# Starting an attention block's second projection inside the hand-ordered opening, with buffers of its own, in a one-core encoder kernel

## The chip, the cores and the metric

The kernel runs on one core of a Trainium2 chip. The core has four compute engines that run side by side and meet at semaphores: TensorE (PE in the profile, its weight loads PEld), VectorE (DVE), ScalarE (ACT) and GpSimd (POOL). SyncE (SP) issues the transfers. The metric is the device time of one execution in microseconds (us). Data that the engines work on lies in SBUF; matmul results land in PSUM, in banks of 2 KB per partition.

## What is computed

A trunk of four residual layers on 512 frames of width 1024, in fp32: pooling mixer, gated MLP, chunked attention with 16 heads, gated MLP. Cut to what matters here:

```python
h = rmsnorm(x, mix_norm[i])
x = x + chunk_attention(h, w_qkv, q_norm, k_norm, rel_table, w_o)   # odd layers
# in it:
qkv = h @ w_qkv
q, k, v = split(qkv, 3)             # q and k: head_rmsnorm, per head
s = q k^T * scale + bias            # then softmax, then p @ v, then @ w_o
# and ahead of it, as behind every mixer:
x = x + (silu(causal_dwconv3(h W_gate)) * (h W_val)) W_out
```

## The kernel before

**Products in parts.** Every fp32 operand of a matmul is split into a hi part (rounded to the type `fp32r`) and a lo part (the rest): ScalarE copies the operand into the hi part, then another engine subtracts it from the raw value to get the lo part. `mm3` (lines 121 to 125) makes a product from three matmuls: hi x hi (L123), lo x hi (L124), hi x lo (L125). So each operand costs a ScalarE copy and a subtraction ahead of its matmuls, and most waits of TensorE are waits for such a part.

**The end of the first MLP** (`output`, lines 785 to 830). The hidden channels are multiplied with `W_out` in four groups. In the last group of layer 0 (`last`, m = 5 blocks of hidden channels) eight output blocks d = 0 to 7 of 128 channels are made one after the other: 15 matmuls into a bank of PSUM, then VectorE adds the bank to `X[d]` (L828). During block d, ScalarE makes the hi part of block d+1's weights (L797); VectorE makes the lo part (`w[d + 1][2]()`, L798) from where TensorE's order has reached the third of the five. Two hooks of the attention block run in here. `after(d - 1)` comes ahead of the matmuls of block d, `amid(d)` ahead of its third set of matmuls. `after` turns the finished block into what the attention needs: `scaled` (three ScalarE instructions: scaled frame values, their hi part, their square), `low` (lo part, VectorE), `add_square`, and every second block `frame_sums` (four VectorE instructions, L957 to L960) and `forms_hi` and `forms_lo` (hi and lo parts of those sums). It also asks for weights (`ask`, `block`).

**The opening of the attention** (`opening`, lines 931 to 1268). Its instructions on TensorE, VectorE, ScalarE and SyncE stay in the order in which the code writes them (`manual_schedule`); GpSimd's are placed by the framework's planner. It makes a first projection of q and k channels (`project(kk)` for four quarters kk of the contraction, whose weights' parts are `q0` to `q3`), then the values v by a Strassen-like scheme in fourteen steps `half(0)` to `half(13)`, each with a hi part (`hi(n)`, L989) and a lo part (`lo(n)`, L992) of its weights. The results stay in two banks at a time (`A`, tag Q; `B`, tag P), and are added up (`add`, L1160) and stored as `V` (`store`: four pairs of a ScalarE hi part, L107, and a VectorE lo part, L108). The opening ends with

```python
half(12, A, "s4", False)
store(y6[0], 2, 0)
half(13, A, "s4", False)
c = pair_of("c12")
nc.scalar.activation(c[0], A[0], AF.Copy)
nc.vector.tensor_copy(c[1], A[1])      # L1264
store(y6[1], 3, 0)
for i in range(2):
    store(c[i], i, 1)
```

**The second projection** (`project(1)` of line 1283, another function of the same name) is a generator that gives one matmul per step, 96 in all: four quarters of 24. Its four results lie in PSUM banks P, P, Q, Q, so the first two need the banks of `B` and the last two those of `A`. `products` loads each quarter with `load_split`: the raw weights into one of three buffers (`wr`), the hi part by ScalarE (L102), the lo part by GpSimd (L103), each into one of two buffers (`wh`, `wl`) that the opening's parts use as well. All raw buffers of the opening's last steps (`b22r`) are among the three.

**The attention loop** (lines 1429 to 1475). For 64 tiles (16 heads of four) it issues scores, turns and mixes. Between them `fill` takes matmuls from a list of fillers, each with its number and the stretch of tiles over which they are spread; the first is `(project(1), 96, -3, 3.5)`. `fill(0)` ahead of the first tile thus takes 45 of the 96. Here only TensorE's order is fixed; the planner places ScalarE's, VectorE's and GpSimd's instructions by its own simulated times, and it may set them between those of the opening.

Of the kernel before, what the change touches and what calls it, by code (L numbers as in the profile page):

```python
# [23 lines left out]
P = 128  # L24
# [48 lines left out]
def trunk(ctx: ExitStack, tc: tile.TileContext, xt, xT, cols, band, edge, poolw, gv, wout, wqk, wv, wo, rel, out):  # L73
# [289 lines left out]
    def ffn(l, first, pool, acc, summed=None, upool=None, hook=None):  # L363
# [421 lines left out]
        def output(g):  # L785
# [24 lines left out]
            for d in range(KD):  # L810
                if d + 1 < KD:
                    halves(d + 1)
                if last and d:
                    hook["after"](d - 1)
                o = psum("Q", f"out{l}_{g}_{d}")
                for i in range(m):
                    if last and i == 2:
                        hook["amid"](d)
                    if i == 2 and d + 1 < KD:
                        w[d + 1][2]()  # L820
                        if d + 1 + ahead < KD:
                            ask(g, d + 1 + ahead)
                        elif d + 2 == KD and g + 2 < len(OUT):
                            ask(g + 1, 0)
                    s = slice(i * P, (i + 1) * P)
                    yield from mm3(o, w[d][0][:, s], w[d][1][:, s], *slot[b + i], i == 0, i == m - 1)
                for fs in (slice(0, S),) if l == 0 or g < len(OUT) - 1 or d < KD - 1 else (slice(0, HALF), slice(HALF, S)):
                    nc.vector.tensor_add(X[d][:, fs], o[:, fs], X[d][:, fs])  # L828
                    if l == 1 and g == len(OUT) - 1:
                        nc.sync.dma_start(out[d * P:(d + 1) * P, fs], X[d][:, fs])  # L830
# [83 lines left out]
    def attention(rest, hook, hidden_slots):  # L914
# [16 lines left out]
        def opening(pre):  # L931
# [91 lines left out]
            def lo(n):  # L1023
                part_lo(f"v{n}")


            def after(d):
                if d in (3, 5):
                    forms_hi((d - 3) // 2)
                scaled(d)  # L1030
                if d == 6:
                    part_hi("q0")
                if d == 1:
                    low(0)
                if d == 2:
                    low(1)
                if d > 1:
                    add_square(d - 1)
                if d in (2, 4, 6):
                    frame_sums(d // 2 - 1)  # L1040
                if d in (3, 5):
                    forms_lo((d - 3) // 2)
                if 3 < d < KD - 1:
                    ask(d - 4)
                if d > 3:
                    for n in (("b11", "b12"), ("b22",), ())[d - 4]:
                        for j in range(2):
                            block(n, j)

            def amid(d):  # L1050
                if d == KD - 1:
                    part_lo("q0")

            hook["after"], hook["amid"] = after, amid
# [10 lines left out]

            def project(kk):
                h, l = part[f"q{kk}"]
                for c, t in [(c, t) for c in range(2) for t in range(TT)] if kk < 3 else [(c, t) for t in range(TT) for c in range(2)]:
                    k = 2 * kk + c
                    q, s = slice(t * P, (t + 1) * P), slice(c * S, (c + 1) * S)  # L1070
                    run(mm3(ov[t], XS[k][:, q], XS[KD + k][:, q], h[:, s], l[:, s], k == 0, k == KD - 1))
# [36 lines left out]
            frame_sums(3)  # L1108
            project(0)
            part_hi("q2")  # L1110
# [5 lines left out]
            t1(0)  # L1116
            project(1)
            part_hi("q3")
# [4 lines left out]
            t2(0)  # L1123
            project(2)
            st = psum("P", "n1_st")
# [12 lines left out]
            lo(0)  # L1138
            project(3)

# [106 lines left out]
            lo(11)  # L1247
            B = [psum("P", f"vd{i}") for i in range(2)]
            half(10, B, "a22", True)
            hi(12)  # L1250
# [4 lines left out]
            hi(13)  # L1255
            lo(13)
            add(y6, B)
            store(y5[1], 3, 1)
            half(12, A, "s4", False)
            store(y6[0], 2, 0)  # L1260
            half(13, A, "s4", False)
            c = pair_of("c12")
            nc.scalar.activation(c[0], A[0], AF.Copy)
            nc.vector.tensor_copy(c[1], A[1])  # L1264
            store(y6[1], 3, 0)
            for i in range(2):
                store(c[i], i, 1)
            return rcol

        def products(ov, w, name, eng=None, evict=None):  # L1270

            for kk in range(4):
                hi, lo = load_split(w[kk], 1024, f"{name}_{kk}", eng=eng)

# [7 lines left out]

        def project(c, banks="PQ"):

# [18 lines left out]

            yield from products(ov, wqk[c], f"wqk{c}", nc.gpsimd, evict)

# [114 lines left out]
        with tc.tile_pool(name="pre", bufs=1, reuse_waits="tile") as pre:  # L1420
            with tc.manual_schedule(engines={ET.PE, ET.DVE, ET.Activation, ET.SP}):
                rcol = opening(pre)
        heads = closing.enter_context(tc.tile_pool(name="bh", bufs=1, reuse_waits="tile"))
# [6 lines left out]
        nb = len(tiles_)  # L1430
        fillers = [(project(1), 96, -3, FE[0]), (project(2), 96, FE[0], FE[1]), (project(3), 96, FE[1], FE[2]), (outputs(), 144, FE[2], nb + FO)]

# [137 lines left out]
```

## Time and profile before

| | us |
|---|---|
| median of three runs | 974.8 (973.29 to 975.76) |
| the profiled execution | 974.83 |
| its span, first to last instruction | 973.0 |
| mean granted TensorE clock | 0.998 |
| share of the span with ScalarE busy | 61% |
| share with GpSimd busy | 10% |

The span is that of one profiled execution. Times in lines of the trace count from the span's start. In a line of the timeline the first number is the start, the second the duration, then engine, line of the code, operation, output<-inputs by the program's names, shapes and count; in brackets the idle time of that engine just ahead, and what ended it. A line of several instructions gives the stretch from the first start to the last end. A busy TensorE row includes the pipeline's depth (0.39 us for a 128x512 matmul that starts every 0.23 us), so TensorE's losses are read from start to start. In a row of the windows stand the length, then TensorE, its weight loads, VectorE, ScalarE and GpSimd (busy us and instructions), the granted TensorE clock, the share of the transfer engines, and GB/s.

### The profile page before, as it was taken

The page shows a single profiled execution, that of the slowest core. Times are in us where ns is not written, and L with a number is a line of the kernel's source. Part 1 is how long each engine was busy: PE and PEld are TensorE (multiplying, and loading weights), DVE is VectorE, ACT ScalarE, POOL GpSimd, SP SyncE. Part 2 cuts the span into 40 slices and gives each one's busy share as a digit, 9 for nine tenths or more (in the row PEclk, how much of TensorE's full clock was granted, in tenths as well). Part 3 has the DMA queues.
Part 4 walks back from the last instruction along what each step waited for, and adds up shares of the span by engine and source line. Part 5 has one row for each costly group of instructions (what it writes and reads, how often), then busy time and mean ns, then how long its engine had stood idle before and what let it go on. Part 6 is the DMA issues. An engine that isn't in the chain of part 4 may idle for free.

```text
span 973.0 us, 13739 instructions
## 1 busy us (share of the span) xinstructions
PE 959.5 (99%) x4958; PEld 811.5 (83%) x4958; DVE 849.5 (87%) x1520; ACT 593.5 (61%) x1023; POOL 96.5 (10%) x83
## 2 busy tenths in 40 slices
PE   8999999999999999998999999999999999999998
PEld 7788988888888877886888787888988888888886
DVE  8999999999899859894677888999999999989953
ACT  7665565654555556464899888646565565556531
POOL 2300000000000000033534443000000000000000
PEclk9999999999999999999999999999999999999999
DMA  8222332332323417013333341332332233322323
GB/s 342 79 90 71 114 114 74 120 119 92 104 76 119 117 41 293 32 44 118 115 116 113 96 115 57 100 93 94 92 115 88 99 122 97 115 99 82 110 80 113
DMA packets 38997, 103.87 MB, mean 107 GB/s; under 512 B 4465, under 2 KB 7937, under 8 KB 38929
## 3 DMA queue, kind: packets, MB, share of 16 engines
q1 hardware_dynamic: 38864, 102.95, 32.7%
q8 instruction: 39, 0.64, 0.3%
q14 instruction: 30, 0.24, 0.1%
q0 software_dynamic: 32, 0.04, 0.0%
q10 hardware_dynamic: 32, 0.00, 0.0%
HBM read 96.65 MB, written 2.14 MB: 102 GB/s over the span
## 4 chain that ended last, share of the span: by engine, by line
PE 92%; DVE 5%; ACT 2%; issue 1%; DMA 0%; DVEq 0%
PE st_m L593 11%; PE out L125 8%; PE out L124 8%; PE out L123 8%; PE st_m L595 6%; PE st_t L593 6%; PE gv L124 4%; PE gv L123 4%; PE gv L125 4%; PE qk L123 3%; PE qk L124 3%; PE qk L125 3%; PE st_t L595 3%; PE st_b L593 3%; DVE one L108 2%; PE tp L1398 2%
## 5 line engine op out<-in xcount | busy, mean ns | idle before, releaser
L124 PE MATMUL out<-one,ow_h 128*128 128x512 f32 x224 | 88.1, 393 | 0.0
L123 PE MATMUL out<-one,ow_h 128*128 128x512 f32 x224 | 88.0, 393 | 0.0
L125 PE MATMUL out<-one,ow_l 128*128 128x512 f32 x224 | 87.9, 393 | 0.0
L828 DVE TENSOR_TENSOR X<-out,X 128x512 f32<-128x512 f32 (+1 forms) x65 | 44.1, 679 | 46.7 <-PE out L125 46.5
L593 PE MATMUL st_m<-two,g_h 128*128 128x512 f32 x240 | 75.0, 394 | 0.0
L593 PE MATMUL st_m<-h,g_h 128*128 128x512 f32 x240 | 74.1, 390 | 0.0
L392 ACT ACTIVATE ow_h<-wo_r 128x768 fp32r<-128x768 f32 (+1 forms) x56 | 44.5, 794 | 43.4 <-PE out L124 40.9
L407 DVE SCALAR_TENSOR_TENSOR c<-a,col,c 128x511 f32<-128x511 f32 (+1 forms) x76 | 56.2, 742 | 0.0
L593 PEld LDWEIGHTS st_m<-h,g_h 128*128 128x128 f32 x240 | 45.1, 188 | 10.3
L595 PEld LDWEIGHTS st_m<-two,g_l 128*128 128x128 f32 x240 | 45.1, 188 | 9.6
L602 ACT ACTIVATE w<-st_m 128x512 f32<-128x512 f32 x30 | 17.9, 598 | 57.1 <-PE st_m L595 57.1
L593 PEld LDWEIGHTS st_m<-two,g_h 128*128 128x128 f32 x240 | 44.1, 188 | 10.1 <-ACT w L602 0.8
L393 DVE TENSOR_TENSOR ow_l<-wo_r,ow_h 128x768 fp32r<-128x768 f32 (+1 forms) x56 | 49.9, 891 | 2.1 <-ACT ow_h L392 2.1
L595 PE MATMUL st_m<-h,g_l 128*128 128x256 f32 x240 | 48.3, 283 | 0.0
L1386 DVE CUSTOM_DVE_ANT_0 sb<-sc,B 128x128 f32<-128x128 f32 (+1 forms) x64 | 31.0, 485 | 19.6 <-PE sc L1383 11.6
L595 PE MATMUL st_m<-two,g_l 128*128 128x256 f32 x240 | 47.6, 280 | 0.0
L124 PEld LDWEIGHTS out<-one,ow_h 128*128 128x128 f32 x224 | 42.4, 189 | 5.6 <-DVE one L418 0.3
L125 PEld LDWEIGHTS out<-one,ow_l 128*128 128x128 f32 x224 | 42.4, 189 | 5.5
L123 PEld LDWEIGHTS out<-one,ow_h 128*128 128x128 f32 x224 | 42.4, 189 | 5.4
L404 ACT ACTIVATE c<-a,col 128x512 f32<-128x512 f32 x38 | 30.7, 812 | 23.2 <-DVE a L751 21.6
L123 PE MATMUL qk<-wqk_h,two 128*128 128x512 f32 x96 | 40.7, 424 | 2.6 <-DVE c L1264 2.6
L1388 ACT ACTIVATE sb<-sb,mx 128x128 f32<-128x128 f32 (+1 forms) x64 | 35.7, 557 | 10.4 <-DVE mx L1386 9.9
(456 smaller groups left out, 3031.3 us busy)
## 6 DMA issues: line engine op xcount, KB each, us to landing
gv_r<-gv SPq DMA_DIRECT2D x86, 512.0 KB, 3.9
wo_r<-wout SPq DMA_DIRECT2D x32, 384.0 KB, 3.1
wo_r<-wout SPq DMA_DIRECT2D x32, 320.0 KB, 2.9
wqk_r<-wqk SPq DMA_DIRECT2D x12, 512.0 KB, 3.4
b<-wv SPq DMA_DIRECT2D x8, 512.0 KB, 6.1
wo_r<-wo SPq DMA_DIRECT2D x8, 512.0 KB, 3.3
xt<-xt SPq DMA_DIRECT2D x4, 512.0 KB, 5.2
X<-xT SPq DMA_DIRECT2D x8, 256.0 KB, 7.4
```

The source lines that it names most:

```text
L123: yield nc.tensor.matmul(o, sh, mh, start=first, stop=False, **how)
L124: yield nc.tensor.matmul(o, sh, ml, start=False, stop=False, **how)
L125: yield nc.tensor.matmul(o, sl, mh, start=False, stop=last, **how)
L392: nc.scalar.activation(hi[:, :n], raw[:, :n], AF.Copy)
L393: return hi, lo, lambda: nc.vector.tensor_sub(lo[:, :n], raw[:, :n], hi[:, :n].bitcast(F32))
L404: nc.scalar.activation(c, a, AF.Identity, scale=cw[2], bias=cw[3])
L407: nc.vector.scalar_tensor_tensor(c[:, j:], a[:, :S - j], cw[2 - j], c[:, j:], op0=OP.mult, op1=OP.add)
L593: nc.tensor.matmul(o, hi[:, c], B[i, name], start=first and i == 0, stop=False, **how)
L595: nc.tensor.matmul(o[:, 0], lo[:, c], B[i, name][:, 0], start=False, stop=i == 3, **how)
L828: nc.vector.tensor_add(X[d][:, fs], o[:, fs], X[d][:, fs])
L1386: nc.vector.tensor_tensor_reduce(out=s_[:, :n], in0=sc[:, :n], in1=BT[h % 2][:, :n][:, ::-1], scale=1.0, scalar=3e38, op0=OP.add, op1=OP.m ...
L1388: nc.scalar.activation(s_[:, :n], s_[:, :n], AF.Exp, scale=-1.0, bias=mx[:, 0:1], accum_out=mx[:, 1:2])
```

## The change

Three things are changed, all between the last output group of the first MLP and the first tile of the attention loop.

In the last output group, the lo part of the next block's weights comes ahead of `frame_sums` and `forms_lo` in VectorE's order, and `part_hi("q0")` comes ahead of `scaled(6)` in ScalarE's order.

```diff
                     if last and i == 2:
-                        hook["amid"](d)
+                        hook["amid"](d, w[d + 1][2] if d + 1 < KD else None)
                     if i == 2 and d + 1 < KD:
-                        w[d + 1][2]()
+                        if not last:
+                            w[d + 1][2]()
...
             def after(d):
+                if d == 6:
+                    part_hi("q0")
                 if d in (3, 5):
                     forms_hi((d - 3) // 2)
                 scaled(d)
-                if d == 6:
-                    part_hi("q0")
-                if d == 1:
-                    low(0)
-                if d == 2:
-                    low(1)
+                if d in (1, 2):
+                    low(d - 1)
                 if d > 1:
                     add_square(d - 1)
-                if d in (2, 4, 6):
-                    frame_sums(d // 2 - 1)
-                if d in (3, 5):
-                    forms_lo((d - 3) // 2)
...
-            def amid(d):
-                if d == KD - 1:
+            def amid(d, low_part):
+                if low_part:
+                    low_part()
+                else:
                     part_lo("q0")
+                d -= 1
+                if d in (2, 4, 6):
+                    frame_sums(d // 2 - 1)
+                if d in (3, 5):
+                    forms_lo((d - 3) // 2)
```

The opening's own `project(kk)` is renamed `query(kk)`. The second projection's generator is started in the opening. Its first quarter gets two buffers of the pool `pre` for its parts (`then`), which ScalarE and VectorE make in the fixed order, and 24 of its matmuls are issued behind `half(13)`. The copies of the last bank come ahead of the stores of `y6`.

```diff
             lo(11)
             B = [psum("P", f"vd{i}") for i in range(2)]
+            raw = load(wqk[1, 0], "wqk1_0_r")
+            then = [pre.tile([P, 1024], F32R, name=f"wqk1_0_{v}", tag="pre", bufs=8) for v in "hl"]
             half(10, B, "a22", True)
...
             hi(13)
             lo(13)
+            nc.scalar.activation(then[0], raw, AF.Copy)
             add(y6, B)
+            nc.vector.tensor_sub(then[1], raw, then[0].bitcast(F32))
+            half(12, A, "s4", False)
             store(y5[1], 3, 1)
-            half(12, A, "s4", False)
-            store(y6[0], 2, 0)
             half(13, A, "s4", False)
             c = pair_of("c12")
             nc.scalar.activation(c[0], A[0], AF.Copy)
             nc.vector.tensor_copy(c[1], A[1])
-            store(y6[1], 3, 0)
+            second = project(1, ready=then)
+            for _ in range(24):
+                next(second)
+            for i in range(2):
+                store(y6[i], 2 + i, 0)
             for i in range(2):
                 store(c[i], i, 1)
-            return rcol
+            return rcol, second
```

`products` takes the ready parts for quarter 0 in place of `load_split`, and the first filler holds the other 72 matmuls, over a stretch that begins later.

```diff
-                hi, lo = load_split(w[kk], 1024, f"{name}_{kk}", eng=eng)
+                hi, lo = ready if ready and kk == 0 else load_split(w[kk], 1024, f"{name}_{kk}", eng=eng)
...
-        fillers = [(project(1), 96, -3, FE[0]), (project(2), 96, FE[0], FE[1]), (project(3), 96, FE[1], FE[2]), (outputs(), 144, FE[2], nb + FO)]
+        fillers = [(second, 72, -1.35, FE[0]), (project(2), 96, FE[0], FE[1]), (project(3), 96, FE[1], FE[2]), (outputs(), 144, FE[2], nb + FO)]
```

More of the change, by code (lines that the diff above doesn't have):

```diff
@@ L1064, in opening, with query @@
             A = [psum("Q", f"va{i}") for i in range(2)]
-            def project(kk):
+            def query(kk):
                 h, l = part[f"q{kk}"]
@@ L1108, in opening @@
             frame_sums(3)
-            project(0)
+            query(0)
             part_hi("q2")
@@ L1116, in opening @@
             t1(0)
-            project(1)
+            query(1)
             part_hi("q3")
@@ L1123, in opening @@
             t2(0)
-            project(2)
+            query(2)
             st = psum("P", "n1_st")
@@ L1138, in opening @@
             lo(0)
-            project(3)
+            query(3)
             ss, a, y, t_ = norms_of(0)
@@ L1264, in opening, with products @@
             nc.vector.tensor_copy(c[1], A[1])
-            store(y6[1], 3, 0)
+            second = project(1, ready=then)
[3 more added lines that the diff above has]
+                store(y6[i], 2 + i, 0)
             for i in range(2):
                 store(c[i], i, 1)
-            return rcol
-        def products(ov, w, name, eng=None, evict=None):
+            return rcol, second
+        def products(ov, w, name, eng=None, evict=None, ready=None):
             for kk in range(4):
-                hi, lo = load_split(w[kk], 1024, f"{name}_{kk}", eng=eng)
+                hi, lo = ready if ready and kk == 0 else load_split(w[kk], 1024, f"{name}_{kk}", eng=eng)
                 for c, t in [(c, t) for c in range(2) for t in range(TT)] if kk < 3 else [(c, t) for t in range(TT) for c in range(2)]:
@@ L1281, in products, with project @@
                         evict(t)
-        def project(c, banks="PQ"):
+        def project(c, banks="PQ", ready=None):
             ov = [psum(banks[t // 2], f"qk{c}_{t}", BANKS[banks]) for t in range(TT)]
@@ L1302, in evict @@
                 late.append(lambda: squares(t))
-            yield from products(ov, wqk[c], f"wqk{c}", nc.gpsimd, evict)
+            yield from products(ov, wqk[c], f"wqk{c}", nc.gpsimd, evict, ready)
             def norms():
@@ L1421, in attention @@
             with tc.manual_schedule(engines={ET.PE, ET.DVE, ET.Activation, ET.SP}):
-                rcol = opening(pre)
+                rcol, second = opening(pre)
         heads = closing.enter_context(tc.tile_pool(name="bh", bufs=1, reuse_waits="tile"))
```

## The prediction

> **What bounds the kernel now.** I read the page first (busy shares, chain), then TensorE's waits, then the order of time on each engine around those waits.
>
> ```profile
> PE 959.5 (99%) x4958; PEld 811.5 (83%) x4958; DVE 849.5 (87%) x1520; ACT 593.5 (61%) x1023; POOL 96.5 (10%) x83
> ...
> PE 92%; DVE 5%; ACT 2%; issue 1%; DMA 0%; DVEq 0%
> ```
>
> TensorE is busy 959.5 of 973.0 us, so an edit that leaves its matmuls alone can gain only at places where TensorE waits. The waits of TensorE between 330 and 460 us, the stretch the diff touches (us in total, times, longest):
>
> ```profile
> PE qk L123 <- DVE c L1264: 2.6, 1, 2.6
> PE qk L124 <- POOL wqk_l L103: 1.2, 1, 1.2
> PE qk L124 <- DVE q_l L992: 0.8, 1, 0.8
> PE out L125 <- DVE ow_l L798: 0.3, 1, 0.3
> PE qk L123 <- ACT q_h L989: 0.2, 1, 0.2
> ```
>
> Five waits at two places: the last three at the end of the first gated MLP ("the front"), the first two where the second projection begins ("the seam"). Their full price is read from TensorE's starts, about 0.23 us apart when nothing is late.
>
> **The front, part by part.** TensorE in order of time (start, duration):
>
> ```profile
> 361.73 0.40 PE L124 MATMUL out<-u0l,ow_h 128*128 128x512 f32 x1
> 362.41 0.50 PE L125 MATMUL out<-u0h,ow_l 128*128 128x512 f32 x1 [0.28 <-DVE ow_l L798]
> ...
> 375.78 0.39 PE L125 MATMUL out<-one,ow_l 128*128 128x512 f32 x1
> 376.35 0.51 PE L123 MATMUL qk<-q_h,two 128*128 128x512 f32 x1 [0.18 <-ACT q_h L989]
> 377.61 0.50 PE L124 MATMUL qk<-q_l,two 128*128 128x512 f32 x1 [0.75 <-DVE q_l L992]
> ```
>
> The three steps are 0.68, 0.57 and 1.26 us instead of 0.23: lost are 0.45 + 0.34 + 1.03 = 1.82 us. What each waits for, on VectorE and ScalarE:
>
> ```profile
> 360.07 0.42 DVE L957 TENSOR_TENSOR s<-y,y 128x256 f32<-128x256 f32 x1
> ...
> 361.54 0.82 DVE L798 TENSOR_TENSOR ow_l<-wo_r,ow_h 128x640 fp32r<-128x640 f32 x1
> ...
> 372.06 0.61 ACT L944 ACTIVATE n_sq<-X 128x512 f32<-128x512 f32 x1
> ...
> 375.26 1.04 ACT L989 ACTIVATE q_h<-wqk 128x1024 fp32r<-128x1024 f32 x1
> ...
> 373.92 0.42 DVE L957 TENSOR_TENSOR s<-y,y 128x256 f32<-128x256 f32 x1
> ...
> 376.33 1.23 DVE L992 TENSOR_TENSOR q_l<-wqk,q_h 128x1024 fp32r<-128x1024 f32 x1 [0.86 <-ACT q_h L989]
> ```
>
> - lo part of `ow` ahead of the frame sums: the four sums stand from 360.07 to 361.54. With the lo part at 360.07 it is done at 360.9; TensorE wants it at 361.96. The 0.45 go.
> - `part_hi("q0")` ahead of `scaled(6)`: ScalarE is free at 372.7, and the buffer that q0 takes over is free once the next-to-last bank has read it, about then. So q_h is done near 373.7 instead of 376.3, and q_l, now behind the square's addition and ahead of the sums, runs from 373.9 to 375.1. The last bank ends at 376.01 less 0.45 = 375.56. The 0.34 and the 1.03 go.
> - What is late next: these sums start 1.2 us later, then the forms made of them, then q1's parts. No instruction is added; lo parts and sums change places. q1's lo part, at 379.40 to 380.6 now, is wanted 24 x 0.23 = 5.5 us after 375.56, at 381.0: about a microsecond to spare. The quarters behind it keep 0.5 to 1.5 us by the same count. SP issues the same transfers at the same points of its order.
>
> Does the gain reach the seam? VectorE itself waits for TensorE ahead of it:
>
> ```profile
> 400.42 0.69 DVE L1176 COPY z<-qk 128x512 f32<-128x512 f32 x1 [1.89 <-PE qk L125]
> 410.00:420.00 10.00, 10.00 (x47) 8.21 (x46) 9.90 (x12) 5.28 (x7) 6.84 (x4) 1.00 0.01 2
> ```
>
> 1.89 us of idle absorb what VectorE is behind. From there to the seam VectorE is full (9.90 of 10 us in the second row, columns PE, PEld, DVE, ACT, POOL), but its start moves with TensorE. I take 1.8 us for the front; bounds 0 (VectorE eats it) and 1.82.
>
> **The seam.** TensorE, VectorE, POOL and ScalarE now:
>
> ```profile
> 439.39 0.39 PE L123 MATMUL qk<-wqk_h,two 128*128 128x512 f32 x1
> 440.96 0.50 PE L124 MATMUL qk<-wqk_l,two 128*128 128x512 f32 x1 [1.18 <-POOL wqk_l L103]
> ...
> 442.68 0.39 PE L125 MATMUL qk<-wqk_h,two 128*128 128x512 f32 x1
> 445.69 0.80 PE L123 MATMUL qk<-wqk_h,two 128*128 128x512 f32 x1 [2.62 <-DVE c L1264]
> ...
> 449.07 0.40 PE L125 MATMUL qk<-wqk_h,two 128*128 128x512 f32 x1
> ...
> 437.46 1.28 DVE L1160 TENSOR_TENSOR y<-y,vd 128x512 f32<-128x512 f32 x2
> 438.65 6.38 DVE L108 SCALAR_TENSOR_TENSOR one<-y,n_y,one 128x128 fp32r<-128x128 f32 x8
> 444.96 0.68 DVE L1264 COPY c<-va 128x512 f32<-128x512 f32 x1
> ...
> 438.54 4.78 POOL L103 TENSOR_TENSOR wqk_l<-wqk_r,wqk_h 128x1024 fp32r<-128x1024 f32 x2 [12.89 <-ACT wqk_h L102]
> ...
> 435.24 1.05 ACT L989 ACTIVATE v_h<-b22r 128x1024 fp32r<-128x1024 f32 x1
> 436.19 1.26 ACT L107 ACTIVATE one<-y,n_y 128x128 fp32r<-128x128 f32 x4
> 439.48 1.04 ACT L102 ACTIVATE wqk_h<-wqk_r 128x1024 fp32r<-128x1024 f32 x1
> ```
>
> From 439.39 to 449.07 are 17 steps, 3.86 us at the 0.227 of undisturbed steps: 5.82 us are lost. 1.34 wait for POOL's lo part, 2.78 for the copy of the last bank, and the rest is a slower clock (PEclk is the column behind POOL):
>
> ```profile
> 446.00:447.00 1.00, 1.00 (x3) 0.81 (x3) 1.00 (x5) 0.95 (x4) 0.00 (x0) 0.50 0.82 304
> 427.83 1.13 DVE L108 SCALAR_TENSOR_TENSOR one<-x,n_y,one 128x128 fp32r<-128x128 f32 x4
> 433.45 0.35 SPq L117 DMA_DIRECT2D wqk_r<-wqk  x1
> wqk_r<-wqk SPq DMA_DIRECT2D x7, 512.0 KB, 3.4
> ```
>
> At a granted 0.50 the 8 steps from 445.69 took 3.38 us instead of 1.82: 1.56. The copy is late because eight store instructions stand ahead of it in 6.38 us; four of them take 1.13 us elsewhere. In between POOL runs two lo parts of 2.4 us, and VectorE hardly gets an instruction through: the two engines hold each other up. [...]
>
> After the change, on the clock of before (all of it comes 1.8 us earlier):
> - The first quarter's raw load is asked behind `channel_major`'s moves, near 427, and lands 3.4 us later. `then[0]` follows hi(13) on ScalarE: 436.2 to 437.2.
> - `then[1]`, on VectorE instead of POOL, comes behind the two additions: 438.74 to 439.95 (1.2 like q_l above). The second matmul wants it at 439.62: a stall of 0.35.
> - ScalarE then makes store(y5[1]) until 438.4. The second quarter's hi part is not in the fixed order; its raw load (433.45 + 3.4) has landed at 436.9. ScalarE is idle until the last bank ends at 439.5, so I put it there, at 438.4, and POOL's lo part behind it from 439.9, when `then[1]` is through, to 442.3.
> - Four store instructions, not eight, now stand ahead of the copy. The first is blocked until 442.3, the others follow; the copy starts at 443.2, and the tenth matmul at 443.95 (0.73 after the copy's start, as now) instead of 445.69.
> - The gap is then 443.95 - 441.8 = 2.15 us, against 2.78. The clock fell behind 2.78 and not behind 1.34. I take it as staying full, since the gap is shorter and TensorE worked just before.
>
> Gain: 445.69 - 443.95 = 1.74, and 1.56 of clock: **3.3 us**. Bounds for the unseen POOL place: the copy unblocked at 441.1 leaves only the 0.35 (gain 5.82 - 0.35 = 5.47); both lo parts in its way again leaves about nothing.
>
> The rest is covered. The planner of matmuls emits 24 of the second projection in the opening and 21 ahead of the first scores, 45 as now. The second quarter is wanted near 447.4 and ready at 442.3. The 16 stores behind the copy (16 x 0.28 from 443.9, and 2.4 for one more POOL part) end near 450.8; VectorE's first need comes later and has room:
>
> ```profile
> 455.96 0.29 DVE L1386 CUSTOM_DVE_ANT_0 sb<-sc,B 128x128 f32<-128x128 f32 x1 [7.17 <-issue]
> PE wo L124 <- DVE two L103: 0.7, 1, 0.7
> PE oo L1410 <- DVE pt1l L103: 0.5, 1, 0.5
> PE tp L1398 <- ACT sb L1390: 0.5, 2, 0.3
> ```
>
> The last three rows are all of TensorE's waits from 449 to 700: behind the seam TensorE alone sets the pace, and what is gained stays.
>
> **Sum.** 1.8 + 3.3 = 5.1 us against 974.83, the profiled execution (span 973.0, 1.8 around it; the median shown is 974.8, the same): **969.7 us**.
>
> **Rivals.**
> 1. POOL's lo part comes behind the copy: 974.83 - 1.8 - 5.47 = **967.6**. For it: ScalarE's queue is filled by a planner whose clock is not the chip's. Against: the idle place ahead of the last copy exists. Chance 0.20.
> 2. The clock falls again, 1.56 us dearer: **971.3**. For: it fell behind 2.78 us. Against: not behind 1.34. Chance 0.13. [...]
> 3. VectorE, full, eats the front's gain: 974.83 - 3.3 = **971.5**. The 1.89 us of idle speak against. Chance 0.05.
> 4. The second quarter's hi part stands behind all stores on ScalarE. No lock then, the copy ends near 441.7, but 16 stores of 0.3 (the row at 436.19) from 440.1 end at 444.9, hi at 445.9, POOL at 448.4 where 445.2 is wanted: 0.35 + 3.2 + 1.56 lost instead of 5.82, the front kept: **972.3**. Chance 0.05.
> 5. Slower: in the attention loop the order of VectorE and ScalarE is planned anew, and each of 16 heads' `mix` waits for its lo part as one does now (0.5): 8.0 - 5.1, **977.7**. It outweighs the gain from 0.32 us a head. For: ScalarE has few gaps there. Against: 0.5 in all now, since parts are made two tiles ahead. Chance 0.07.
>
> My forecast has 0.50; with it goes POOL's lo part getting ahead of `then[1]`, which stalls the second matmul until 441.95 and costs nearly the same (969.6).
>
> **Chances.** A measurement of this kernel tells some 0.3% (2.9 us) from no change. Faster: the forecast, rival 1 and half of 2, 0.77. Within: the other half, 3 and 4, 0.16. Slower: 0.07. The range, 967.0 to 972.5, reaches from just under rival 1 to just over rival 4.
>
> **What would show it.** TensorE's list of waits loses ow_l L798, q_l L992 and q_h L989; q_h precedes y L941 in ScalarE's order; a 128x1024 subtraction at the seam is VectorE's; the copy of the last bank follows four stores; a wait of some 2 us for it remains, with a POOL part beside it, and PEclk stays 1.00. Wrong would be: any of the three still there, the copy unblocked (rival 1), a clock of 0.50 (2), or new waits at oo (5).

## The result and the profile after

The changed kernel takes 969.56 us (median; 969.34 to 969.78, 4 executions) against 975.09 us before (973.29 to 975.76, 4 executions, one more than in the table above): a ratio of 0.9946, 95% interval 0.9929 to 0.9963. The profiled execution after took 969.34 us with a span of 967.5 us, 5.49 us less than the profiled one of before.

The page of the changed kernel, busy time by engine and the shares of the chain that ended last:

```profile
PE 957.4 (99%) x4958; PEld 810.7 (84%) x4958; DVE 850.8 (88%) x1521; ACT 593.7 (61%) x1023; POOL 94.6 (10%) x82
...
PE 94%; DVE 3%; ACT 2%; issue 0%; DMA 0%; DVEq 0%
```

One subtraction went from POOL to VectorE (83 to 82 instructions, 1520 to 1521), TensorE does as many matmuls as before, and VectorE's share of the chain falls from 5% to 3%. TensorE's waits of the changed kernel between 330 and 700 us (total, times, longest):

```profile
PE qk L123 <- DVE c L1269: 1.7, 1, 1.7
PE wo L124 <- DVE two L103: 0.6, 1, 0.6
PE oo L1419 <- DVE pt1l L103: 0.5, 1, 0.5
PE tp L1407 <- ACT sb L1399: 0.5, 2, 0.3
```

Of the five waits at the front and the seam one is left, that for the copy of the last bank. The other three rows are those that already stood behind the seam, the same to 0.1 us: the attention loop was not replanned for the worse (rival 5).

The end of the first MLP in the timeline of the changed kernel (start, duration), TensorE, VectorE, ScalarE:

```profile
361.61 0.40 PE L124 MATMUL out<-u0l,ow_h 128*128 128x512 f32 x1
361.85 0.40 PE L125 MATMUL out<-u0h,ow_l 128*128 128x512 f32 x1
...
375.12 0.39 PE L125 MATMUL out<-one,ow_l 128*128 128x512 f32 x1
375.35 0.39 PE L123 MATMUL qk<-q_h,two 128*128 128x512 f32 x1
375.58 0.39 PE L124 MATMUL qk<-q_l,two 128*128 128x512 f32 x1
...
359.96 0.82 DVE L798 TENSOR_TENSOR ow_l<-wo_r,ow_h 128x640 fp32r<-128x640 f32 x1
...
373.27 1.22 DVE L993 TENSOR_TENSOR q_l<-wqk,q_h 128x1024 fp32r<-128x1024 f32 x1
...
371.92 1.04 ACT L990 ACTIVATE q_h<-wqk 128x1024 fp32r<-128x1024 f32 x1
372.86 0.71 ACT L942 ACTIVATE y<-X,col 128x512 f32<-128x512 f32 x1
```

The three steps that were late are 0.23 to 0.24 us now. The lo part of `ow` runs 1.6 us earlier than before, and q_h and q_l are done over a microsecond before TensorE wants them.

The seam in the timeline of the changed kernel, TensorE, VectorE, POOL, ScalarE:

```profile
437.30 0.39 PE L123 MATMUL qk<-wqk_h,two 128*128 128x512 f32 x1
437.77 0.50 PE L124 MATMUL qk<-wqk_l,two 128*128 128x512 f32 x1
...
439.51 0.40 PE L125 MATMUL qk<-wqk_h,two 128*128 128x512 f32 x1
441.56 0.50 PE L123 MATMUL qk<-wqk_h,two 128*128 128x512 f32 x1 [1.66 <-DVE c L1269]
...
443.51 0.39 PE L125 MATMUL qk<-wqk_h,two 128*128 128x512 f32 x1
...
436.50 1.22 DVE L1263 TENSOR_TENSOR wqk_l<-wqk_r,wqk_h 128x1024 fp32r<-128x1024 f32 x1
437.63 3.27 DVE L108 SCALAR_TENSOR_TENSOR one<-y,n_y,one 128x128 fp32r<-128x128 f32 x4
440.83 0.68 DVE L1269 COPY c<-va 128x512 f32<-128x512 f32 x1
441.43 4.32 DVE L108 SCALAR_TENSOR_TENSOR one<-y,n_y,one 128x128 fp32r<-128x128 f32 x8
...
437.33 2.64 POOL L103 TENSOR_TENSOR wqk_l<-wqk_r,wqk_h 128x1024 fp32r<-128x1024 f32 x1 [13.84 <-PE va L1096]
442.21 2.61 POOL L103 TENSOR_TENSOR wqk_l<-wqk_r,wqk_h 128x1024 fp32r<-128x1024 f32 x1 [2.23 <-ACT wqk_h L102]
...
436.15 1.05 ACT L102 ACTIVATE wqk_h<-wqk_r 128x1024 fp32r<-128x1024 f32 x1
```

VectorE makes the first quarter's lo part; four stores, lengthened from 1.13 to 3.27 us by the POOL part beside them, stand ahead of the copy; the copy holds up the tenth matmul. From the first to the eighteenth matmul the seam takes 443.51 - 437.30 = 6.21 us instead of 9.68. Behind the gap the clock is full (the stretch in the windows of the changed kernel; PEclk behind POOL):

```profile
446.00:447.00 1.00, 1.00 (x6) 0.84 (x5) 1.00 (x6) 0.00 (x0) 0.00 (x0) 1.00 0.42 130
```

**Where the 5.5 us of span come from:** 0.12 us of difference stands already at 347 us, ahead of everything that was changed; 1.91 comes at the front (from the `u0l` matmul at 347.76 us before and 347.64 after to the first q_l matmul, at 377.61 and 375.58, are 29.85 and 27.94 us); 3.47 at the seam. The two matmuls from which the front is counted, in the kernel before and in the changed one:

```profile
347.76 0.40 PE L124 MATMUL out<-u0l,ow_h 128*128 128x512 f32 x1
...
347.64 0.40 PE L124 MATMUL out<-u0l,ow_h 128*128 128x512 f32 x1
```

Of the seam's, 2.04 lies up to the tenth matmul (445.69 - 439.39 = 6.30, now 441.56 - 437.30 = 4.26), and 1.43 in the eight steps behind it (3.38, now 1.95), which is the clock.

No edit of this document changes the code ahead of that matmul, yet in the twelve profiled executions shown here it starts at 347.62 to 349.48 us. So below, what an edit is worth at the seam is checked against steps inside an execution, since a difference of two spans may hold up to 1.9 us of something else.

In the sections below, "gap" is TensorE's step to the matmul that waits for the copy, less the 0.23 us of an undisturbed step: 2.78 us before, 2.05 - 0.23 = 1.82 after. "Half clock" is the stretch of a granted 0.50 behind a gap; in the trace of before it lasts 3.4 us, from 445.4 to 448.8, and begins 0.3 us ahead of the matmul that ends the gap. It shows in a whole execution too: those 3.4 us at 0.50 take 0.0017 off the mean granted clock of a span of 973 us, so a mean of 0.998 or less is read here as an execution with it, and 0.999 or more as one without.

### The profile page after: what moved, and what is told of

It reads as the page before. It is cut to its first block, busy times and chain, and to the rows that moved or that the text cites. A ratio compares the mean times of both kernels' runs of the same rounds, so it can differ in the third digit from the quotient of the medians.

```text
span 967.5 us, 13741 instructions
## 1 busy us (share of the span) xinstructions
PE 957.4 (99%) x4958; PEld 810.7 (84%) x4958; DVE 850.8 (88%) x1521; ACT 593.7 (61%) x1023; POOL 94.6 (10%) x82
## 4 chain that ended last, share of the span: by engine, by line
PE 94%; DVE 3%; ACT 2%; issue 0%; DMA 0%; DVEq 0%
PE st_m L593 11%; PE out L124 8%; PE out L123 8%; PE out L125 8%; PE st_m L595 6%; PE st_t L593 6%; PE gv L124 4%; PE gv L123 4%; PE gv L125 4%; PE qk L123 3%; PE qk L124 3%; PE qk L125 3%; PE st_t L595 3%; PE st_b L593 3%; PE tp L1407 2%; PE oo L1419 2%
```

## Experiments

Each kernel was timed in five rounds against the kernel before on the same chip; a result is the median, the range and the number of executions, then the ratio to the kernel before with its 95% interval. E1 to E4, E5 to E8, and E9 and E10 ran on three chips. On each of them the executions of the kernel before without the half clock have a median of 973.64 to 973.66 us, so that times may be compared from one to another. Diffs are against the changed kernel unless another is named. The theory on trial is the prediction's own: a front term, a copy that is late because of the stores and POOL ahead of it, and a clock that falls behind a long gap. Its rivals here: that one edit carries it all, that VectorE eats the front's gain, or that the own buffers, not the place of the copy, make the seam.

**E1, the front alone.** The opening's end, the generator and the fillers as in the kernel before:

```diff
-            nc.scalar.activation(then[0], raw, AF.Copy)
             add(y6, B)
-            nc.vector.tensor_sub(then[1], raw, then[0].bitcast(F32))
-            half(12, A, "s4", False)
             store(y5[1], 3, 1)
+            half(12, A, "s4", False)
+            store(y6[0], 2, 0)
             half(13, A, "s4", False)
...
-        fillers = [(second, 72, -1.35, FE[0]),
+        fillers = [(project(1), 96, -3, FE[0]),
```

> Only the front is changed (lo part of the next weights ahead of the frame sums, q0's parts ahead of scaled(6)); the second projection starts as before. Theory (two separate gains that add): the three waits at ow_l, q_h and q_l go, TensorE is some 1.9 us earlier at the seam, the seam's loss of 5.8 us stays with its half clock: 975.1 - 1.9 = 973.2. Rival (VectorE is full, the front's gain is eaten on the way to the seam): 975.1, with new waits of TensorE between 376 and 437.

Measured: 973.01 us (971.49 to 974.33, 12); 0.9981 [0.9973, 0.9990]. TensorE's waits of E1 between 330 and 460 us:

```profile
PE qk L123 <- DVE c L1266: 2.6, 1, 2.6
PE qk L124 <- POOL wqk_l L103: 1.2, 1, 1.2
```

The forecast's front term alone gives 974.83 - 1.8 = 973.0. The three waits of the front are gone, the two of the seam as long as before. The front took the same 27.94 us as after, and from there to the first matmul of the second projection it is 61.67 us (61.78 before, 61.72 after), so VectorE does not eat the gain. The range is wide for a reason that the clock shows: eight of the twelve executions have a mean granted clock of 0.998 or less and took 973.0 to 974.3 us, the other four 971.5 to 972.0.

**E2, the seam alone.** `output`, `after` and `amid` as in the kernel before, the rest as changed:

```diff
-                        hook["amid"](d, w[d + 1][2] if d + 1 < KD else None)
+                        hook["amid"](d)
...
-                if d == 6:
-                    part_hi("q0")
                 if d in (3, 5):
                     forms_hi((d - 3) // 2)
                 scaled(d)
+                if d == 6:
+                    part_hi("q0")
```

> Only the seam is changed (own buffers, parts in the fixed order, 24 matmuls in the opening, copies of the last bank ahead of the stores of y6); the front is as before. Theory: the three waits of the front stay (1.9 us), the seam loses 0.2 + 1.8 us and no clock: 975.1 - 3.5 = 971.6. Rival (the two parts need each other, since the seam's ready parts are late when TensorE comes later or earlier): gains of E1 and E2 together differ from 5.5 by more than 1.

Measured: 971.73 us (971.32 to 972.70, 6); 0.9972 [0.9960, 0.9984]. The forecast's seam term alone gives 974.83 - 3.3 = 971.5. The three waits of the front are back at 0.8, 0.3 and 0.2 us, the wait for the copy is 1.7 us, and no execution has a clock under 0.999. Counted from the median of the kernel before on that chip, 974.61 us, E1 and E2 gain 1.6 and 2.9 us. Together that is 4.5 us, a microsecond less than 5.5, which is the mark that the expectation set for its rival. But this median mixes executions with and without the half clock. Counted from those with it alone (975.28 us), E1's with it (973.28) gain 2.0 us and E2 3.55, together 5.55. The steps say the same: E1's front is that of the changed kernel, and E2's gap is 1.84 us against 1.82. So the two halves of the change are separate.

**E3, the copy ahead of the four stores that are left.** The lo parts of `store(y5[1])` move behind the copy on VectorE; ScalarE's order stays:

```diff
             half(12, A, "s4", False)
-            store(y5[1], 3, 1)
+            store(y5[1], 3, 1, False)
             half(13, A, "s4", False)
             c = pair_of("c12")
             nc.scalar.activation(c[0], A[0], AF.Copy)
             nc.vector.tensor_copy(c[1], A[1])
+            store(y5[1], 3, 1, True)
```

(`False` leaves the lo parts out, `True` makes only them.)

> The changed kernel, but VectorE copies the second half of the last bank ahead of the four lo parts of the store of y5[1] too (ScalarE's hi parts stay where they are). POOL's lo part of the second quarter still runs at the same place. Theory (the wait of 1.8 us is the queue of four stores behind POOL's part, ahead of the copy): the copy starts right behind the own lo part, the wait for it goes, TensorE ends 1.8 us earlier, 967.7; the stores end as late as before and nobody waits for them. Rival (the pace behind the seam is set by the stores, or by ScalarE): the wait at the copy goes but comes back later, 969.5.

Measured: 967.54 us (967.41 to 967.89, 4); 0.9926 [0.9913, 0.9939]. VectorE and POOL in the timeline of E3:

```profile
437.69 0.68 DVE L1273 COPY c<-va 128x512 f32<-128x512 f32 x1
438.29 4.79 DVE L1173 SCALAR_TENSOR_TENSOR one<-y,n_y,one 128x128 fp32r<-128x128 f32 x12
...
437.39 2.65 POOL L103 TENSOR_TENSOR wqk_l<-wqk_r,wqk_h 128x1024 fp32r<-128x1024 f32 x1 [13.84 <-ACT wqk_h L102]
442.27 5.15 POOL L103 TENSOR_TENSOR wqk_l<-wqk_r,wqk_h 128x1024 fp32r<-128x1024 f32 x1 [2.24 <-ACT wqk_h L102]
```

The copy, which reads PSUM, takes 0.68 us beside the POOL part (437.39 to 440.04 us), as it does with none beside it (at 440.83 us in the changed kernel), and TensorE has no wait left at the seam. Why it is not held up there and a store is, no run shows. The 2.0 us against the changed kernel are the wait that was left, a gap of 1.82 us.

**E4, POOL's part behind the copy (rival 1 made to happen).** The second quarter's load and hi part may be issued only after ScalarE's copy `c[0]`:

```diff
-            nc.scalar.activation(c[0], A[0], AF.Copy)
+            first_copy = nc.scalar.activation(c[0], A[0], AF.Copy)
...
-            second = project(1, ready=then)
+            second = project(1, ready=then, behind=first_copy)
...
-                hi, lo = ready if ready and kk == 0 else load_split(...)
+                with tc.issue_after(behind.ins) if behind and kk == 1 else nullcontext():
+                    hi, lo = ready if ready and kk == 0 else load_split(...)
```

> The changed kernel, but the second quarter's hi part (and so POOL's lo part) is put behind the copy of the first half of the last bank on ScalarE; VectorE's order is untouched, four stores still stand ahead of the copy. Theory (POOL's part is what holds the first of the four stores for some 2.1 us): the four stores take 1.1 us instead of 3.3, the copy ends 2.1 us earlier, no wait for it is left; the second quarter's lo part comes at about 443.4 where 443.2 is wanted, so up to 0.3 us may be lost there: 967.7 to 968.0. Rival (VectorE's own work sets the copy's time, POOL only stands beside it): the four stores still take about 3 us, 969.5.

Measured: 969.65 us (969.17 to 970.70, 5); 0.9949 [0.9937, 0.9961]. No gain over the changed kernel, against 967.7 to 968.0 expected. VectorE, POOL and TensorE in the timeline of E4:

```profile
438.27 1.14 DVE L108 SCALAR_TENSOR_TENSOR one<-y,n_y,one 128x128 fp32r<-128x128 f32 x4
439.32 0.68 DVE L1269 COPY c<-va 128x512 f32<-128x512 f32 x1
439.92 2.18 DVE L108 SCALAR_TENSOR_TENSOR one<-y,n_y,one 128x128 fp32r<-128x128 f32 x8
442.02 1.13 DVE L108 SCALAR_TENSOR_TENSOR one<-c,n_y,one 128x128 fp32r<-128x128 f32 x4
...
445.44 0.50 PE L124 MATMUL qk<-wqk_l,two 128*128 128x512 f32 x1 [1.30 <-POOL wqk_l L103]
```

and the POOL part by itself (the window of E4 from 441 to 444 us):

```profile
441.64 3.74 POOL L103 TENSOR_TENSOR wqk_l<-wqk_r,wqk_h 128x1024 fp32r<-128x1024 f32 x1 [17.52 <-DVE one L108]
```

Half of the theory held: without POOL beside them the four stores take 1.14 us and the copy is not awaited. But the wait moved. VectorE runs twelve more stores without a break until 443.15, and the POOL part that begins at 441.64 is done at 445.38, 2.2 us after that run has ended and not 2.4 after its start. TensorE waits 1.3 us for it.

**E5, eight stores ahead of the copy again.** The own buffers stay; `store(y6[0])` returns ahead of the copies:

```diff
             store(y5[1], 3, 1)
+            store(y6[0], 2, 0)
             half(13, A, "s4", False)
...
-            for i in range(2):
-                store(y6[i], 2 + i, 0)
+            store(y6[1], 3, 0)
```

> The changed kernel with the stores in their old order: store(y6[0]) ahead of the copies again, so eight store instructions, not four, stand ahead of the second copy; own buffers and the 24 matmuls in the opening stay. Theory (POOL's one part costs 2.1 us once, each further store 0.27): the copy comes 1.1 us later than in the changed kernel, 970.6, with a gap of 2.9 us on TensorE, as long as the one before the change, so that some executions also have the half clock (+1.6): single times from 970.6 to 972.2. Rival (the order of copies and stores is what the change gains at the seam, the buffers do little): the whole seam comes back, 973.0, as in E1.

Measured: 975.08 us (974.16 to 976.92, 11); 1.0004 [0.9995, 1.0013]. With the front's gain in it, this seam is slower than that of the kernel before. The expectation, 970.6 to 972.2, missed by 3 us; the rival's 973.0 missed too. The timeline of E5, VectorE, POOL and TensorE:

```profile
438.67 6.41 DVE L108 SCALAR_TENSOR_TENSOR one<-y,n_y,one 128x128 fp32r<-128x128 f32 x8
445.00 0.68 DVE L1270 COPY c<-va 128x512 f32<-128x512 f32 x1
...
438.37 2.64 POOL L103 TENSOR_TENSOR wqk_l<-wqk_r,wqk_h 128x1024 fp32r<-128x1024 f32 x1 [13.84 <-PE va L1096]
442.07 2.34 POOL L103 TENSOR_TENSOR wqk_l<-wqk_r,wqk_h 128x1024 fp32r<-128x1024 f32 x1 [1.06 <-ACT wqk_h L102]
...
445.73 0.80 PE L123 MATMUL qk<-wqk_h,two 128*128 128x512 f32 x1 [4.79 <-DVE c L1270]
```

The eight stores last long enough to meet the third quarter's POOL part as well: two parts stand in the copy's way, as before the change. TensorE's losses of 1.34 and 2.78 us in the kernel before become one gap of 4.95. The mean granted clock is 0.997 or less in all eleven executions.

**E6, the place of the copies alone.** The kernel before, with one move:

```diff
             half(12, A, "s4", False)
-            store(y6[0], 2, 0)
             half(13, A, "s4", False)
...
-            store(y6[1], 3, 0)
+            for i in range(2):
+                store(y6[i], 2 + i, 0)
```

> The kernel before with one edit: the copies of the last bank ahead of the stores of y6. No own buffers, POOL makes the first quarter's lo part as before, the front is as before. Theory (two lo parts of POOL let through hardly two instructions of VectorE, so the copy still waits for the end of the second): four stores fewer are worth 4 x 0.27 = 1.1 us at the copy, and TensorE waits 1.2 us for POOL's first part as before: 974.6 - 1.0 = 973.6, with the half clock in some executions. Rival (the order alone brings most of the seam): 971.5.

Measured: 972.57 us (972.37 to 973.68, 10); 0.9978 [0.9969, 0.9987]. VectorE and TensorE in the timeline of E6:

```profile
438.77 5.34 DVE L108 SCALAR_TENSOR_TENSOR one<-y,n_y,one 128x128 fp32r<-128x128 f32 x4
444.03 0.68 DVE L1263 COPY c<-va 128x512 f32<-128x512 f32 x1
...
444.76 0.50 PE L123 MATMUL qk<-wqk_h,two 128*128 128x512 f32 x1 [1.57 <-DVE c L1263]
```

Four stores behind two POOL parts still take 5.34 us. Counted from the first matmul of the second projection (439.54 us here, 439.39 before), the copy comes 1.08 us earlier than in the kernel before, as expected, and the gap is 1.73 us instead of 2.78. The time is a microsecond better than expected because no execution of ten has a mean clock under 0.999: against the kernel before without the half clock, 973.65 us, E6 gains just the 1.08.

**E7, twelve stores ahead of the copy.** E5, with `store(y6[1])` moved up too:

```diff
             store(y5[1], 3, 1)
+            for i in range(2):
+                store(y6[i], 2 + i, 0)
             half(13, A, "s4", False)
...
-            for i in range(2):
-                store(y6[i], 2 + i, 0)
```

> The changed kernel with both stores of y6 ahead of the copies: twelve store instructions ahead of the second copy. Made to see what a longer gap on TensorE costs. The copy comes 2.1 us later than in the changed kernel, and up to 2.4 more if POOL's next part falls in: gap 3.9 to 6.3 us. Theory (the clock falls to half for some 3 us in a share of the executions that grows with the gap): 971.7 to 974.1 without, 1.6 more with the half clock, in most executions. Rival (the clock does not depend on the gap): a spread as small as in the changed kernel, granted clock 1.000 throughout.

Measured: 976.25 us (975.37 to 977.23, 11); 1.0013 [1.0004, 1.0021], slower than the kernel before. The twelve stores take 7.47 us, 1.1 more than E5's eight, which is four of 0.27 us. TensorE's longer wait in the timeline of E7 (the matmul ahead of it starts at 442.47 us):

```profile
447.60 0.80 PE L123 MATMUL qk<-wqk_h,two 128*128 128x512 f32 x1 [4.73 <-DVE c L1271]
```

The gap, 5.13 - 0.23 = 4.90 us, lies in the 3.9 to 6.3 expected, and all executions have the half clock. The time is still above the expected 971.7 to 974.1 and 1.6 more: a second loss of 1.01 us was not in the sum, the wait for ScalarE's copy, which has four more hi parts ahead of it.

**E8, both first.** E3, and `then[1]` ahead of the additions:

```diff
-            add(y6, B)
             nc.vector.tensor_sub(then[1], raw, then[0].bitcast(F32))
+            add(y6, B)
```

> E3 (copy ahead of all stores on VectorE), and the first quarter's own lo part ahead of the two additions of y6. The second matmul of the projection waits 0.24 us for that lo part in E3; now it is ready and the additions free their banks in time (the first at about 437.0 for 437.3, the second at 437.7 for 438.0). Theory: no wait is left at the seam, 967.3, 0.2 under E3. Rival (the additions come too late for the first matmul): as E3 or 0.3 worse, with a wait of TensorE for y L1162.

Measured: 967.50 us (967.13 to 967.67, 5); 0.9923 [0.9910, 0.9935]. The same as E3 within what can be measured: the step to the second matmul, 0.53 us in E3, becomes 0.31, and that is all.

**E9, E5 with the third quarter's POOL part out of the way.** Tests the reason given for E5's miss: the third quarter's load and hi part are issued only after ScalarE's last store.

```diff
             store(y5[1], 3, 1)
+            store(y6[0], 2, 0)
             half(13, A, "s4", False)
...
-                hi, lo = ready if ready and kk == 0 else load_split(...)
+                with tc.issue_after(hook["stored"].ins) if ready and kk == 2 else nullcontext():
+                    hi, lo = ready if ready and kk == 0 else load_split(...)
```

> E5 again (eight stores ahead of the second copy), but the third quarter's hi part is put behind the last store on ScalarE, so that POOL's second lo part cannot start ahead of the copy. Theory (E5 was 5 us dearer than the changed kernel because the copy, 1.1 us later, fell behind POOL's second part too, 2.3 us, and the long gap brought the half clock every time): the eight stores take 4.3 us instead of 6.4, the copy starts 2 us earlier than in E5, the gap on TensorE is 2.9 us; 970.7 without the half clock, 972.3 with it, both among the executions. Rival (the second half of the eight stores is slow of itself, say by ScalarE's hi parts): 975.0 as E5.

Measured: 972.48 us (971.87 to 973.50, 11); 0.9980 [0.9972, 0.9989]. VectorE in the timeline of E9:

```profile
438.15 4.33 DVE L108 SCALAR_TENSOR_TENSOR one<-y,n_y,one 128x128 fp32r<-128x128 f32 x8
442.40 0.68 DVE L1271 COPY c<-va 128x512 f32<-128x512 f32 x1
```

and TensorE at the gap:

```profile
440.01 0.40 PE L126 MATMUL qk<-wqk_h,two 128*128 128x512 f32 x1
443.14 0.50 PE L124 MATMUL qk<-wqk_h,two 128*128 128x512 f32 x1 [2.73 <-DVE c L1271]
```

The same eight stores take 4.33 us instead of 6.41, and the gap is 3.13 - 0.23 = 2.90 us instead of 4.95. So 2.05 us of E5's miss were the second POOL part. The rest, under a microsecond, is not traced; E5's profiled execution was already 1.0 us later than that of the changed kernel ahead of the front. The gap of 2.9 us brings the half clock in eleven executions of eleven, where some without it were expected.

**E10, the place of the copy without own buffers.** The front, and E3's order of copy and stores; the second projection starts as in the kernel before, POOL making the first lo part:

```diff
-            raw = load(wqk[1, 0], "wqk1_0_r")
-            then = [pre.tile(...) for v in "hl"]
...
-            nc.scalar.activation(then[0], raw, AF.Copy)
             add(y6, B)
-            nc.vector.tensor_sub(then[1], raw, then[0].bitcast(F32))
+            store(y5[1], 3, 1, False)
             half(12, A, "s4", False)
-            store(y5[1], 3, 1)
             half(13, A, "s4", False)
             c = pair_of("c12")
             nc.scalar.activation(c[0], A[0], AF.Copy)
             nc.vector.tensor_copy(c[1], A[1])
-            second = project(1, ready=then)
-            for _ in range(24):
-                next(second)
+            store(y5[1], 3, 1, True)
...
-        fillers = [(second, 72, -1.35, FE[0]),
+        fillers = [(project(1), 96, -3, FE[0]),
```

> The front as changed, and VectorE's copy of the last bank ahead of all stores as in E3, but no own buffers, no fixed order for the first quarter's parts and no matmuls in the opening: POOL makes the first quarter's lo part. Theory (the order of the copies carries the seam; the own buffers are worth only the 1.3 us that TensorE waits for POOL's first lo part, less the 0.3 it waits for the own one): no wait for the copy, one of 1.2 us for wqk_l, 967.5 + 1.0 = 968.5. Rival (own buffers and matmuls in the opening are worth more than that first wait): 970 or above, with other waits.

Measured: 968.69 us (968.49 to 969.04, 5); 0.9942 [0.9928, 0.9956]. TensorE's only wait of E10 between 330 and 460 us:

```profile
PE qk L124 <- POOL wqk_l L103: 1.2, 1, 1.2
```

So the own buffers, with their parts in the fixed order and the 24 matmuls in the opening, are worth 968.69 - 967.54 = 1.15 us beside E3. That is the wait: the step to the second matmul is 1.61 us in E10 and 0.53 in E3. The place of the copy carries the rest of the seam. With the front and nothing else (E1) the time is 973.01: moving the copies alone takes 4.3 us off it, 2.8 of them the gap and the other 1.5 the half clock, which E1's median contains.

## Why the prediction was right

969.7 us were forecast and 969.56 measured, and the steps are those of the forecast. That the two agree so closely is in part luck: the sizes at the seam were off by +0.30 and -0.13 us, and the profile that the sum starts from happened to have the half clock.

- **The front:** 1.82 us from the starts of three steps, 1.91 measured. The bound "VectorE eats it" did not come in: the seam's first matmul starts 2.09 us earlier, of which the front's gain and the early 0.12 are 2.03 (rival 3). One margin was misread: q1's lo part, done at 380.6 and wanted at 381.0, had 0.4 us to spare and not a microsecond. It did no harm, since that part came 1.6 us earlier too (377.79 us instead of 379.40).
- **The place of POOL's part:** forecast in ScalarE's idle place ahead of the last copy; it is there (hi part from 436.15 to 437.20, POOL from 437.33, a little ahead of the end of `then[1]` at 437.72 and not behind it), and the four stores are held up as forecast. That the first of them would be blocked until POOL's part ends was the author's estimate from the rows of before, where eight stores took 6.38 us beside two parts that kept their 2.4 us each; in the changed kernel the first store took 2.49 us and ended at 440.12, POOL's part at 439.97. The copy came 0.86 us behind POOL's end, forecast 0.9. `then[1]` and POOL's part end 0.1 and 0.2 us earlier than forecast, counted from the first matmul, and that makes 2.04 us of the forecast 1.74.
- **The clock:** 1.56 us forecast, 1.43 measured between the two profiled executions. But the term was taken for a property of the kernel before, and it is not one of every execution. In 59 executions of the kernel before beside the experiments, 34 have a mean clock of 0.998 or less (median 975.26 us) and 25 have 0.999 or more (median 973.65): the 1.6 us between the two is this term. Both kinds occur on each of the three chips (9 of 18, 18 of 26 and 7 of 15 with the half clock). Against the second kind the change is worth 973.65 - 969.56 = 4.1 us. The profile from which the sum was made is of the first kind, and the median of before is among them. From a profile of the second kind the same steps without the clock give an estimate of 973.65 - 1.8 - 1.74 = 970.1.
- **What was summed as one:** the prediction counted the move from eight to four stores and the move of the first lo part off POOL together. E5, E6 and E10 part them: the own buffers without the copies' move (E5) make it 2.1 us slower than the old seam (E1), the copies' move without the buffers gains 0.22% (E6), and both are needed for a gap of 1.82 us with no wait for POOL ahead of it. Put ahead of all stores, the copy alone leaves no gap (E10).
- **A rival's price was wrong.** Rival 1 had the copy unblocked with the 0.35 us wait of `then[1]` as the only loss left, 967.6. E4 made it happen and got 969.65: with POOL's part moved away from four stores it met the next twelve, and the wait went to the second quarter. That quarter was counted as ready with five microseconds to spare, which is true only of the other place. 967.5 is reached by moving the copy, not POOL (E3, E8).
- **The other rivals.** Rival 2 did not come in: the mean granted clock of the changed kernel is 1.000 in all four executions. Rival 4 did not either, since POOL's part stands where it was forecast; its price was not tried.

E3 and E8 beat both kernels, by 0.74% and 0.77% against the one before; E3 needs the fewer moves. With no TensorE wait left from the front to the first scores, little more is to be had there by order alone: E8's steps to the second and third matmul, 0.31 and 0.24 us, are all that is late.

## What to carry to other kernels

When a short instruction that frees a PSUM bank stands behind longer work that another engine can hold up (four stores of 1.13 us took 3.27 beside a POOL part), move that instruction ahead of the work before giving the work buffers of its own; here the order was worth about four microseconds, the half clock included (E1 to E10), and the buffers one (E10 to E3). A part of another engine that is pushed out of one run of instructions can land in the next, as in E4, where TensorE then waited 1.30 us for it; so look up what stands there. And a stall a few microseconds long can cost its own length and a stretch of half clock behind it, in some executions (42 of 71 at a gap of 2.78 us) or in all (33 of 33 in E5, E7 and E9, at 2.9 us and more): compare many executions, and ask of a single profile which kind it is.

## What the hardware showed beyond the forecast

**The half clock goes with the length of the gap, and at one length it comes in some executions only.** Executions with a mean granted clock of 0.998 or less, by the longest gap in the kernel's profile (in E4 and E10 that is the wait for POOL's part):

| gap, us | kernels | with half clock |
|---|---|---|
| 1.38 to 1.84 | after, E2, E4, E6, E10 | 0 of 30 |
| 2.78 | before, E1 | 42 of 71 |
| 2.9 | E9 | 11 of 11 |
| 4.95 and about 4.9 | E5, E7 | 22 of 22 |

At 2.78 us it costs about 1.6 us (975.26 against 973.65 in the kernel before). The runs do not show where between 1.84 and 2.78 us it begins, nor why 2.9 us brings it every time and 2.78 does not. The sum of neighbouring gaps does not decide it: E6 has two, 1.31 and 1.73 us with eight matmuls between them, together more than E9's one of 2.90, and never the half clock.

**A POOL part is either let in at once or held off to the end of a run, as these rows show it.** In the changed kernel the first store beside the POOL part takes 2.49 us where such a store takes 0.28 (the window from 437.6 to 439.9 us):

```profile
437.63 2.49 DVE L108 SCALAR_TENSOR_TENSOR one<-y,n_y,one 128x128 fp32r<-128x128 f32 x1
```

There VectorE waited and POOL hardly did (2.64 us; the six such parts from 452 to 492 us in the kernel before take 2.39 to 2.41). In E3 the second part (442.27, 5.15 us) begins in the middle of a run of stores that all keep 0.27 us, and ends 2.2 us after the run has (the window of E3 from 441 to 446 us; the first row holds the last eight of the twelve stores shown above):

```profile
440.90 2.18 DVE L1173 SCALAR_TENSOR_TENSOR one<-y,n_y,one 128x128 fp32r<-128x128 f32 x8
443.00 2.18 DVE L1173 SCALAR_TENSOR_TENSOR one<-c,n_y,one 128x128 fp32r<-128x128 f32 x8
```

E4 (3.74 us) and E8 (4.92) show the same, and so do parts that meet the end of a run in E9 (3.04) and E10 (2.76): in all five kernels the part ends 2.2 to 2.3 us after the last store of the run, as if it had started there. The changed kernel's second part (442.21, 2.61 us) begins inside a run of stores too and is let in; the eight stores beside it take 4.32 instead of 2.18 us. In E3 POOL's part was held off over some ten stores (2.9 us at 0.27 each). What decides between the two stays open.
